# A hybrid decoder layer on one core: SBUF tiles moved by 96 bytes on the left and by 32 bytes on the right

## The chip, the cores and the metric

The kernel runs on one core of a Trainium2 chip. The metric is the device time of one execution, in microseconds. TensorE (PE, with its weight loads shown apart as PEld), VectorE (DVE), ScalarE (ACT) and GpSimd (POOL) compute; SyncE (SP) issues most DMAs.

## The reference

One decoder layer for 1,024 rows of 1,024 numbers in float32:

```
x = x + 0.5 * swiglu(rms_norm(x, g_ffn1), w1_gate, w1_up, w1_down)     # inner width 2816
h = rms_norm(x, g_mix);  proj = h @ w_in                               # one combined projection
y_a = top-k sparse attention: indexer scores, 256 keys of each row, softmax, latent values
y_b = stick-breaking attention (cumulative sums instead of a softmax)
x = x + (sigmoid(g_a) * (y_a @ w_o_a) + sigmoid(g_b) * (y_b @ w_o_b)) @ w_out
x = x + 0.5 * swiglu(rms_norm(x, g_ffn2), w2_gate, w2_up, w2_down)
swiglu(h, g, u, d) = (silu(h @ g) * (h @ u)) @ d
```

## The kernel before, in words

A float32 product is made of three TensorE products: each operand is split into a high part and the rest, and high by high, high by rest and rest by high are added up in PSUM. Most of the work is of one form, a matmul of 128 x 128 numbers that are loaded as weights (the stationary operand, a slice of 512 bytes of each partition) by 512 columns that stream past them (the moving operand, 2,048 bytes of each partition). There are 8,196 of them among the 10,460 matmuls. While one matmul streams, the weights of the next are loaded.

The stages in order are: the first feed-forward block, its entry (`ffn_in`, matmuls at L463 to L465) and its exit (`ffn_out`, L672 to L674); the projections and both attentions, woven together by a planner (L226 to L1950; transposes and products of many shapes); the output projections; and the second feed-forward block by the same two functions. In the feed-forward blocks both products are made by a Strassen scheme on half matrices: `ffn_in` makes seven products of 12 matmuls for each pair of column blocks and each of gate and up, so the loop is seven products of 12 matmuls, over and over, with sums between them on VectorE.

Where a tile lies in SBUF is set by pools. Each partition is filled from both ends: a pool opened with `side="right"` takes its bytes below the last right pool, the others take theirs above the last left one. Pools of small tiles come first on the left (`cst`, `small`), and each small tile takes 32 bytes or a multiple. Nearly all large tiles are of 2,048 or 4,096 bytes, so that all of them on one side begin at one place within every 512 bytes. In the program before, the large tiles of the left begin at place 352 (the first at byte 20,320 = 39 x 512 + 352), those of the right at place 480 (the last at byte 225,248 = 439 x 512 + 480). Both places are 32 bytes past a multiple of 64. Four slots of 4,224 bytes on the right begin at 480, 96, 224 and 352: they hold the weights of the latent queries and keys (`wuqh` at 96, `wqih` at 224).

Which side an operand is on follows from its pool. In `ffn_in` the moving operands (`aB`, `aT`) come from the right pool `t1`. The stationary operands come from `op`, which deals out tiles of two pools in turn, four of the right pool `outer` (`wt`, L256 to L257) and five of the left pool `ring1`, nine in a round:

```
op = in_turn((wt, 4), (lambda name: pool.tile([P, 1024], F32R, tag="r", name=name, bufs=NR), NR))
```

In `ffn_out` both operands (`aA` or `aS`, and `aB` or `aT`) come from `op`. The VectorE's tiles `ay`, `as`, `au` come from left pools, `x` of the first block from the right. In the attention stage, score rows, queries and values lie on both sides. PSUM tiles and DRAM tensors lie elsewhere and are no part of this.

Of the kernel before, what the change touches and what calls it, by code (L numbers as in the profile page):

```python
# [10 lines left out]
F32 = mybir.dt.float32  # L11
# [12 lines left out]
P = 128  # L24
# [220 lines left out]
def trunk(ctx, tc, x, positions, g_ffn1, w1_gate, w1_up, w1_down, g_mix, w_in, g_cq, w_uq_a, w_q_idx,  # L245
          g_q_a, g_k_a, w_uv_a, w_o_a, w_o_b, w_out, g_ffn2, w2_gate, w2_up, w2_down, inv_freq, out):
    nc = tc.nc
    cst = ctx.enter_context(tc.tile_pool(name="cst", bufs=1))
    small = ctx.enter_context(tc.tile_pool(name="small", bufs=4))
    dram = ctx.enter_context(tc.tile_pool(name="dram", bufs=1, space=DRAM))  # L250
    outer = ctx.enter_context(tc.tile_pool(name="outer", bufs=1, side="right"))

    def rawt(name):
# [11 lines left out]
        return small.tile([P, n], dt, name=name, bufs=bufs)  # L265


    ident = cst.tile([P, P], F32, name="ident")
    make_identity(nc, ident)
    mhalf = cst.tile([P, H], F32, name="mhalf")  # L270
# [1836 lines left out]
```

## Time and profile before

| | us |
|---|---|
| median of 3 runs | 2323.19 (2322.38 to 2325.25) |
| the profiled execution | 2324.09 |
| its span, first to last instruction | 2322.3 |
| PE busy in the span | 2211.2 |
| DVE, ACT, POOL busy | 1590.9, 1114.3, 881.6 |

The profiled execution is one run of the program; its span leaves out about 1.8 us around the first and the last instruction. In the rows below a group of instructions stands with its line, engine, operation and tiles (output <- inputs, buffer numbers left out), and then with times. A matmul's own duration contains the time that its last columns take through the array, so a row of matmuls overlaps: its pace is read from the starts, or from how many fill a stretch.

### The profile page before, as it was taken

How to read it: one execution, taken by the hardware profiler on the slowest of the kernel's cores; microseconds unless marked ns; L12 is line 12 of the kernel's file. 1: busy time of each engine (PE TensorE's matmuls, PEld its weight loads, DVE VectorE, ACT ScalarE, POOL GpSimd, SP SyncE). 2: the span in 40 equal slices, each digit the busy share in tenths (PEclk: the TensorE clock that was granted, in tenths of full speed). 3: DMA queues.
4: the chain of work that ended last, by engine and by line, in shares of the span. 5: the costliest groups of instructions: out<-in, count | busy, mean ns of one | idle time of the engine just before them, and what ended most of it. 6: DMA issues, size and time to landing. Idle time of an engine off the chain costs nothing.

```text
span 2322.3 us, 30186 instructions
## 1 busy us (share of the span) xinstructions
PE 2211.2 (95%) x10460; PEld 1811.4 (78%) x10460; DVE 1590.9 (69%) x2512; ACT 1114.3 (48%) x2133; POOL 881.6 (38%) x648
## 2 busy tenths in 40 slices
PE   7999999999999898889999699999999999999999
PEld 6788888878879777667788578877878888888877
DVE  5765656678862897666698877862476565667685
ACT  4323232334452479889988456633342323233443
POOL 3555555432252444211122133146245555542233
PEclk9999999999999999999999799999999999999999
DMA  5232323587664243645454533357313333358755
GB/s 165 75 114 91 114 87 116 159 307 241 168 208 116 81 132 98 163 98 128 109 138 120 172 109 97 128 178 254 118 59 109 96 107 98 105 163 291 234 168 181
DMA packets 252538, 330.64 MB, mean 142 GB/s; under 512 B 20577, under 2 KB 155377, under 8 KB 252385
## 3 DMA queue, kind: packets, MB, share of 16 engines
q1 hardware_dynamic: 235264, 288.83, 41.4%
q0 software_dynamic: 7488, 24.16, 2.7%
q10 hardware_dynamic: 9632, 15.73, 2.0%
q8 instruction: 82, 1.34, 0.2%
q14 instruction: 72, 0.58, 0.1%
HBM read 234.78 MB, written 93.88 MB: 142 GB/s over the span
## 4 chain that ended last, share of the span: by engine, by line
PE 70%; DVE 11%; ACT 9%; DMA 4%; issue 4%; POOL 1%; ACTq 0%; SPq 0%; DVEq 0%; POOLq 0%
PE p L673 5%; PE p L674 5%; PE p L672 5%; ACT junka L1127 4%; PE pc L463 3%; PE pc L465 3%; PE pc L464 3%; PE pd L465 3%; PE pd L463 3%; PE pd L464 3%; PE pa L463 3%; PE pa L465 3%; PE pa L464 3%; PE pb L463 2%; PE pb L465 2%
## 5 line engine op out<-in xcount | busy, mean ns | idle before, releaser
L1127 ACT ACTIVATE junka<-u,cand,sig 128x1024 bf16<-128x1024 f32 (+5 forms) x186 | 182.7, 982 | 22.1 <-DVE cand L1124 10.0
L1563 DVE TENSOR_TENSOR_SCAN left<-left 128x640 f32<-128x640 f32 (+3 forms) x64 | 92.7, 1449 | 3.8 <-ACT left L1555 3.8
L1612 DVE TENSOR_TENSOR pt<-pstT,pt 128x512 fp32r<-128x512 f32 (+1 forms) x96 | 51.3, 551 | 22.0 <-ACT pt L1610 21.4
L1664 PE MATMUL pstT<-ident,sa 128*128 128x128 f32 x288 | 47.4, 279 | 13.7 <-DVE pt L1612 12.0
L1729 DVE CUSTOM_DVE_ANT_0 e<-psL,bias 128x512 f32<-128x512 f32 (+3 forms) x96 | 49.4, 549 | 14.4 <-PE psL L1766 14.4
L1612 DVE TENSOR_TENSOR pt<-pspT,pt 128x512 fp32r<-128x512 f32 x72 | 46.5, 683 | 18.2 <-ACT pt L1610 18.2
L1741 ACT ACTIVATE e<-e,nm 128x256 f32<-128x256 f32 (+7 forms) x64 | 49.4, 774 | 18.5 <-DVE nm L1736 17.3
L1820 PE MATMUL pspT<-ident,e 128*128 128x128 f32 x288 | 42.0, 285 | 16.2 <-DVE ri L1743 9.2
L1566 DVE TENSOR_TENSOR sa<-sa,left 128x639 f32<-128x639 f32 (+3 forms) x64 | 53.1, 829 | 5.0 <-ACT sa L1557 1.8
L1664 PEld LDWEIGHTS pstT<-ident,sa 128*128 128x128 f32 x288 | 35.1, 142 | 26.2 <-DVE pt L1612 17.5
L673 PE MATMUL p<-bT,bS 128*128 128x512 f32 x132 | 51.8, 392 | 2.7 <-DVE bT L374 2.7
L1631 POOL DMA_DIRECT2D ybld<-yl x16 | 8.8, 551 | 118.8 <-DVE yl L1629 66.3
L1610 ACT ACTIVATE pt<-pspT 128x512 fp32r<-128x512 f32 x72 | 39.5, 596 | 29.8 <-PE pspT L1820 29.5
L673 PE MATMUL p<-aT,aS 128*128 128x512 f32 x132 | 51.8, 393 | 1.1 <-DVE aT L374 1.1
L1820 PEld LDWEIGHTS pspT<-ident,e 128*128 128x128 f32 x288 | 35.3, 146 | 22.5 <-DVE e L1744 9.5
L674 PE MATMUL p<-bT,bS 128*128 128x512 f32 x132 | 51.5, 393 | 0.8 <-POOL bS L374 0.8
L1610 ACT ACTIVATE pt<-pstT 128x512 fp32r<-128x512 f32 (+1 forms) x96 | 46.7, 501 | 11.6 <-PE pstT L1664 10.0
L1476 DVE SCALAR_TENSOR_TENSOR u<-relu,WI,u 128x512 f32<-128x512 f32 (+1 forms) x70 | 49.5, 727 | 3.9 <-ACT relu L1469 2.7
L674 PE MATMUL p<-aT,aS 128*128 128x512 f32 x132 | 50.9, 393 | 0.0
L1557 ACT ACTIVATE sa<-psz 128x512 f32<-128x512 f32 (+2 forms) x96 | 47.0, 503 | 5.0 <-ACT evg L1060 2.4
L1555 ACT ACTIVATE left<-psz 128x512 f32<-128x512 f32 (+2 forms) x96 | 45.4, 497 | 8.4 <-PE psz L1590 3.0
L1469 ACT ACTIVATE relu<-psdot 128x512 f32<-128x512 f32 (+1 forms) x80 | 40.0, 521 | 16.5 <-DVE u L1476 10.6
(3061 smaller groups left out, 8315.3 us busy)
## 6 DMA issues: line engine op xcount, KB each, us to landing
aw<-in_w_down_dram SPq DMA_DIRECT2D x33, 512.0 KB, 4.6
bw<-in_w_down_dram SPq DMA_DIRECT2D x33, 512.0 KB, 4.5
a0r<-in_w_gate_dram SPq DMA_DIRECT2D x22, 512.0 KB, 4.2
a1r<-in_w_up_dram SPq DMA_DIRECT2D x22, 512.0 KB, 4.7
b0r<-in_w_gate_dram SPq DMA_DIRECT2D x22, 512.0 KB, 4.1
b1r<-in_w_up_dram SPq DMA_DIRECT2D x22, 512.0 KB, 4.9
x<-in_x_dram SPq DMA_DIRECT2D x16, 512.0 KB, 6.5
gd<-evg ACTq DMA_DIRECT2D x32, 256.0 KB, 2.9
```

What stands on the lines that cost most here:

```text
L463: nc.tensor.matmul(ps, a[:, c], b[k][:, HI], start=start and k == 0, stop=False, skip_group_check=True)
L464: nc.tensor.matmul(ps, a[:, c], b[k][:, LO], start=False, stop=False, skip_group_check=True)
L465: nc.tensor.matmul(ps, a[:, l], b[k][:, HI], start=False, stop=k == 3, skip_group_check=True)
L672: nc.tensor.matmul(ps[q][m], S[:, h], T[:, HI], start=p == 0, stop=False)
L673: nc.tensor.matmul(ps[q][m], S[:, h], T[:, LO], start=False, stop=False)
L674: nc.tensor.matmul(ps[q][m], S[:, l], T[:, HI], start=False, stop=p == last)
L1127: nc.scalar.activation(junks[1][:, 0:(i + 1) * P], score[i], AF.Sign, scale=sig[:, b:b + 1], bias=cand.bitcast(F32)[:, b:b + 1], accum_out ...
L1563: nc.vector.tensor_tensor_scan(back, back, back, 1.0, op0=ALU.mult, op1=ALU.bypass)
L1610: nc.scalar.activation(pt[:, off:512], tp[:, off:512], AF.Copy)
L1612: nc.vector.tensor_sub(pt[:, 512 + off:1024], tp[:, off:512], f32(pt[:, off:512]))
L1664: nc.tensor.transpose(tp[:, q * P:(q + 1) * P], A[n + q][:, j * P:(j + 1) * P], ident)
L1820: nc.tensor.transpose(tp[:, q * P:(q + 1) * P], E[n + q][:, j * P:(j + 1) * P], ident)
```

## The change

Two unused tiles are allocated before all others. On the right one of 8 numbers (32 bytes of each partition) ahead of pool `outer`; on the left one of 24 numbers (96 bytes) as the first of `cst`. Nothing reads or writes them. All left tiles move up by 96 bytes, all right tiles down by 32. The large tiles of both sides then begin at place 448 within 512 (352 + 96, and 480 - 32), a whole multiple of 64. The small left tiles, which follow each other at 32 bytes, move by the same 96; the slots of 4,224 bytes on the right go to 448, 64, 192 and 320. Every engine's instructions, their order and their waits are those of before; their SBUF addresses alone differ.

```
@@ -248,6 +248,8 @@
     cst = ctx.enter_context(tc.tile_pool(name="cst", bufs=1))
     small = ctx.enter_context(tc.tile_pool(name="small", bufs=4))
     dram = ctx.enter_context(tc.tile_pool(name="dram", bufs=1, space=DRAM))
+
+    ctx.enter_context(tc.tile_pool(name="edge", bufs=1, side="right")).tile([P, 8], F32, name="edger")
     outer = ctx.enter_context(tc.tile_pool(name="outer", bufs=1, side="right"))
@@ -265,6 +267,7 @@
         return small.tile([P, n], dt, name=name, bufs=bufs)
 
+    cst.tile([P, 24], F32, name="edgel")
     ident = cst.tile([P, P], F32, name="ident")
     make_identity(nc, ident)
```

## Rows read from the trace of the kernel before

**Rows 1.** The page: span, and busy time of each engine.
```profile
span 2322.3 us, 30186 instructions
PE 2211.2 (95%) x10460; PEld 1811.4 (78%) x10460; DVE 1590.9 (69%) x2512; ACT 1114.3 (48%) x2133; POOL 881.6 (38%) x648
```

**Rows 2.** The page: the chain that ended last, shares by engine.
```profile
PE 70%; DVE 11%; ACT 9%; DMA 4%; issue 4%; POOL 1%; ACTq 0%; SPq 0%; DVEq 0%; POOLq 0%
```

**Rows 3.** Windows by stage: stretch, its length, busy us (and instructions) of engines, DMA.
```profile
0.00:120.00 120.00, 103.25 (x493) 85.14 (x494) 80.39 (x107) 51.06 (x90) 49.33 (x44) 1.00 0.41 122
120.00:462.60 342.60, 342.60 (x1485) 279.16 (x1484) 214.05 (x236) 104.04 (x178) 174.96 (x121) 1.00 0.35 113
462.60:689.10 226.50, 223.20 (x981) 180.92 (x980) 178.39 (x253) 103.66 (x182) 76.19 (x49) 1.00 0.72 226
689.10:1655.00 965.90, 885.06 (x4614) 730.68 (x4613) 677.73 (x1400) 625.98 (x1285) 293.89 (x245) 0.97 0.46 134
1655.00:1715.00 60.00, 60.00 (x312) 50.45 (x311) 36.60 (x50) 24.10 (x44) 18.50 (x14) 1.00 0.16 49
1715.00:2095.60 380.60, 378.03 (x1637) 307.33 (x1636) 245.03 (x267) 114.17 (x196) 198.63 (x137) 1.00 0.36 115
2095.60:2322.30 226.70, 219.03 (x949) 177.71 (x947) 158.69 (x205) 91.23 (x160) 70.12 (x42) 1.00 0.66 219
```

**Rows 4.** Instructions by tile: one product, two rounds; count, ns min/median/max, first and last start.
```profile
L463 PE MATMUL pb<-aT,a04S x4: 392/394/404, 202.2 to 204.3; 128*128 128x512 f32 x4
L464 PE MATMUL pb<-aT,a04S x4: 390/394/404, 202.4 to 204.5; 128*128 128x512 f32 x4
L465 PE MATMUL pb<-aT,a04S x4: 392/394/397, 202.7 to 204.8; 128*128 128x512 f32 x4
...
L463 PE MATMUL pb<-aT,a14S x4: 389/389/389, 221.6 to 223.6; 128*128 128x512 f32 x4
L464 PE MATMUL pb<-aT,a14S x4: 389/389/389, 221.8 to 223.9; 128*128 128x512 f32 x4
L465 PE MATMUL pb<-aT,a14S x4: 389/389/396, 222.0 to 224.1; 128*128 128x512 f32 x4
```

**Rows 5.** Windows of unbroken rows of matmuls: length, PE busy (matmuls), clock, DMA.
```profile
2276.48:2287.42 10.95, 10.95 (x49) 1.00 0.47 146
2287.42:2298.62 11.19, 11.19 (x49) 1.00 0.99 351
...
324.10:332.23 8.13, 8.13 (x36) 1.00 0.60 177
1840.62:1848.75 8.13, 8.13 (x36) 1.00 0.61 179
1538.42:1559.97 21.55, 21.55 (x96) 1.00 0.43 135
507.99:513.58 5.59, 5.59 (x25) 1.00 1.02 389
513.58:521.82 8.24, 8.24 (x37) 1.00 0.95 318
```

**Rows 6.** Windows of two rows of matmuls with 256 columns.
```profile
689.28:700.68 11.39, 11.39 (x97) 1.00 0.79 271
759.13:762.72 3.59, 3.59 (x32) 1.00 0.11 24
```

**Rows 7.** Instructions by tile: matmuls of the latent queries, both operands on the right.
```profile
L306 PE MATMUL psq<-wuqh,cql x16: 388/392/404, 800.8 to 928.4; 128*128 128x512 f32 x16
...
L306 PE MATMUL psq<-wqih,cql x12: 387/389/395, 763.2 to 852.0; 128*128 128x512 f32 x12
```

**Rows 8.** Instructions by line: sums on DVE, tiles on either side.
```profile
L431 DVE TENSOR_TENSOR ay<-x,ay x8: 679/682/684, 39.5 to 55.9; 128x512 f32<-128x512 f32 x8
...
L431 DVE TENSOR_TENSOR ay<-ay,ay x4: 678/682/682, 61.4 to 63.2; 128x512 f32<-128x512 f32 x4
L431 DVE TENSOR_TENSOR ay<-x x4: 678/679/679, 63.8 to 65.6; 128x512 f32<-128x512 f32 x4
```

**Rows 9.** Instructions by tile: splits on ACT and POOL, tiles on either side.
```profile
L373 ACT ACTIVATE a02A<-a0r x3: 615/632/634, 101.0 to 110.9; 128x512 fp32r<-128x512 f32 x3
L374 POOL TENSOR_TENSOR a02A<-a0r,a02A x3: 1291/1304/1307, 102.5 to 111.6; 128x512 fp32r<-128x512 f32 x3
```

**Rows 10.** The page, DMA issues: weights of the two blocks, us to landing.
```profile
a0r<-in_w_gate_dram SPq DMA_DIRECT2D x22, 512.0 KB, 4.2
...
b0r<-in_w_gate_dram SPq DMA_DIRECT2D x22, 512.0 KB, 4.1
```

**Rows 11.** Timeline of PE: every third matmul of the key projection; start, us.
```profile
728.80 0.28 PE L304 MATMUL pska<-wka0h,mhi 128*128 128x264 f32 x1
...
729.17 0.28 PE L304 MATMUL pska<-wka0h,mhi 128*128 128x264 f32 x1
...
729.53 0.28 PE L304 MATMUL pska<-wka0h,mhi 128*128 128x264 f32 x1
...
729.89 0.28 PE L304 MATMUL pska<-wka1h,mhi 128*128 128x264 f32 x1
```

More of the change, by code (lines that the diff above doesn't have):

```diff
@@ L250, in trunk @@
     dram = ctx.enter_context(tc.tile_pool(name="dram", bufs=1, space=DRAM))
+    ctx.enter_context(tc.tile_pool(name="edge", bufs=1, side="right")).tile([P, 8], F32, name="edger")
     outer = ctx.enter_context(tc.tile_pool(name="outer", bufs=1, side="right"))
@@ L265, in sm @@
         return small.tile([P, n], dt, name=name, bufs=bufs)
+    cst.tile([P, 24], F32, name="edgel")
     ident = cst.tile([P, P], F32, name="ident")
```

## The prediction

> **What bounds the kernel now.** I read the busy times first: PE is busy 95% of the span, the next engine 69% [rows 1]. Then the chain of waits that ended last: 70% of it is PE, 4% DMA [rows 2]. Then the same by stage [rows 3]. The reader is to see that PE has no gap at all in the entry of the first feed-forward block after its opening (342.60 of 342.60 us), next to none in that of the second (60.00 of 60.00, 378.03 of 380.60), and few in the exits (223.20 of 226.50, 219.03 of 226.70). Only in the attention stage does it stand still for long (80.8 of 965.9 us). So in 1,236 of 2,322 us the time is the number of matmuls by the pace at which they follow each other, and whatever changes that pace changes the time. The granted clock is at its upper level (1.00) in all of these stages, so the pace isn't the clock's.
>
> The pace isn't constant. One product of `ffn_in`, with the same moving tiles, lasts 389 ns a matmul in one round and 392 to 394 in another [rows 4]. The sole difference is the tile of the stationary operand: in the built program `a14S` of this product starts at byte 208,864 (place 480 within 512, as the moving tiles), `a04S` at 32,608 (place 352). Longer rows say it with starts. In the exit of the second block, 48 matmuls with both operands at one place fill 10.95 us, 228.1 ns each; the next 48, with operands 128 apart, 11.19 us, 233.1 ns (a window counts one matmul more, whose end reaches into it) [rows 5]. The other windows there are pairs against the DMAs: 35 matmuls 128 apart take 232.3 ns at a DMA share of 0.60 or 0.61, 36 at one place 228.9 ns at 0.95, 24 apart 232.9 ns at 1.02, 95 at one place 226.8 ns at 0.43. So it's the place and not the traffic.
>
> Is it the side or the place? The two latent-query products answer: all their operands are on the right. `wuqh` is at 96 and `cql` at 480, 384 apart, and the median matmul takes 392 ns; `wqih` is at 224, 256 apart, 389 ns [rows 7]. So 0 and 256 apart are the fast distances, 128 and 384 the slow ones, on either side. I laid the trace's matmuls beside the built program's addresses, in order: over all rows without a gap, 226 or 227 ns is the commonest interval at 0 or 256 (mean 228.4 ns of some 4,500), and hardly ever occurs at 128 or 384 (mean 232.5 of 3,355). An interval is also slow when only the next matmul's weights, loaded while this one streams, are apart.
>
> **The change part by part.** Instructions, order and waits stay, so nothing is added on any queue and no wait is new. All that can change is how long an instruction or transfer takes at its new address.
>
> 1. Matmuls of 512 columns. After the change both sides are at place 448, so every pair of large tiles is 0 apart. Intervals that are slow now, counted in program order by the places of the two operands and of the next weights: 1,111 in the first entry, 347 in the first exit, 518 between the blocks, 1,123 and 352 in the second entry and exit, 3,451 of 8,195. Each loses what divides the two means of its stage: 4.3 ns in the entries, 4.3 in the exits (232.6 less 228.3), sizes that lie between those of [rows 4] and [rows 5], and 2.6 between. That is 4.8, 1.5, 1.3, 4.8 and 1.5 us, 13.9 us of PE time. A few pairs of `psq` stay 128 apart (both on the right, moved alike); they aren't worth a term.
>
> How much of it reaches the end: in the first entry all but the opening's share (225 slow intervals before 120 us, 1.0 us, half of which I leave to the waits there), 4.3; in the second 4.6 of 4.8; in the exits 1.3 each, as PE stands still for 3.3 and 7.7 us there and a wait for a load eats what comes before it; between the blocks 0.5 of 1.3, since there ACT and DVE hold much of the chain. Sum 12.0 us. What is late next in the entries? Nothing near: DVE is busy 214 of 342.6 us there, POOL 175, DMA 0.35 [rows 3], and 3.4 us less changes that by 1%.
>
> 2. Matmuls of 256 columns and transposes: nothing. 96 matmuls with operands 384 apart fill 11.39 us (118.7 ns), 30 at one place 3.59 us (119.6) [rows 6]; at 256 columns distance costs nothing.
>
> 3. DVE, ACT and POOL: nothing. Sums whose inputs lie on two sides take 682 ns at the median, on the left alone 682, on the right alone 679 [rows 8]; the splits, written to either side, spread by 19 and 16 ns [rows 9]. The small tiles swap places (those at 32 past a 64 go to whole 64 and the others the reverse), half of them in each class as now.
>
> 4. DMAs: no large transfer of before starts at whole 64, so this has no row. DMA holds 4% of the chain, 93 us [rows 2]. Two equal sets of loads land in 4.2 and 4.1 us [rows 10]; that much (2.4%) of 93 us is 2.2 us either way. I take 0, as most of it is hidden, and keep both ends.
>
> 5. Place 448 itself. Two operands at one place give the same pace at 352 as at 480, but both are 32 past a 64. Bounds: the best product runs at 226.8 ns throughout [rows 5], so if all went so, another 1.6 ns x 8,195 x 0.87 (the share that reaches the end in 1) = 11.4 us would go; if all went at the slow pace, 4.1 ns x 4,744 x 0.87 = 16.9 us would come on top of now. I take the present mean: the key projection steps its moving operand through places 0, 32 and 64 past, every second at whole 64, and three matmuls take 0.37, 0.36 and 0.36 us [rows 11].
>
> The profiled execution took 2324.09 us, 0.90 above the median. 2324.09 - 12.0 = 2312.1; for the median 2323.19 - 12.0 = 2311.2 us.
>
> A rule speaks against all this. The Trainium skill, "SBUF — State Buffer", section "Who interferes with whom", gives PE two read ports, one for the moving operand and one for the weights, independent of each other, and says that PE never waits on anyone; by it the place of the two can't matter and the sum is 0, 2323.2 us. The trace disagrees for 512 columns (228.1 and 233.1 ns) and agrees for 256 (118.7 and 119.6); the measurement decides.
>
> **The rivals.**
>
> A. The pace doesn't depend on the place but on something that goes with it, say the distance of the bytes or the pool, and stays: 2323 us, within 2. For it: nearly all slow pairs are left with right. Against it: the pairs on the right alone, 384 and 256 apart, and fast pairs that lie 100 KB from each other (`aT` at 90,080 to 200,672 with `a14S` at 208,864 [rows 4]). The rule of the Trainium skill above would give this time as well.
>
> B. Slower: whole 64 is a bad place for PE to read two streams from. It decides in the feed-forward blocks: if matmuls at one place ran above 230.2 ns, the mean of now over both kinds (4,744 x 228.4 + 3,451 x 232.5, over 8,195), all would be lost; at 232.5 the time is 2323.2 + 16.9 = 2340 us. For it: no row has both 512-column operands there. Against it: rows 11, and the equal pace at 352 and 480.
>
> C. PE gains, and waits take more of it: staged loads and PSUM readers in the exits and the attention come when they come, the exits and everything between give nothing, and of the entries two thirds: 6 us, 2317 us. For it: the idle time of the exits [rows 3]. Against it: the first entry's 342.60 of 342.60.
>
> D. More: the slow intervals left at one place (231 to 236 ns) go as well, 2311.2 - 11.4 = 2300 us. Nothing speaks for it but that 64 is a rounder place.
>
> **How the numbers follow.** Forecast 0.75 (2307 to 2315: 16.1 us off, which is 13.9 with the DMA's 2.2, to 8, two thirds of 12.0), A 0.10, B 0.05, C 0.07, D 0.03. A measurement of this kernel tells 0.2% from no change, 4.6 us. Faster by more: the forecast, C and D, 0.85; within 0.2%: A, 0.10; slower: B, 0.05. The range takes the forecast and C and some way to the others: 2304 to 2319.
>
> **What would show it.** In the profile after, `pb<-aT,a04S` at a median of 389 like `a14S`, and the window of the 48 matmuls that took 11.19 us at 10.95; PE busy lower by some 12 us at the same count; the first entry's 342.6 us shorter by 3.4 or more; 256-column rows, DVE, ACT and POOL groups as now. The forecast is wrong if the 392 to 394 stay (A), if rows that stood at 389 rise (B), or if PE's busy time falls and the span doesn't (C).

## The result, and the profile after

The changed kernel takes 2302.22 us (median of 4 runs, 2298.46 to 2305.05); the kernel before, run beside it, took 2323.34 us (2322.38 to 2325.25). The ratio is 0.9907 (95% interval 0.9890 to 0.9924): 21 us faster, where the forecast was 12 us and its range ended at 2304.

The page of the changed kernel, span, busy times and the chain's shares, against [rows 1, 2]:

```profile
span 2298.7 us, 30186 instructions
PE 2188.0 (95%) x10460; PEld 1808.7 (79%) x10460; DVE 1590.1 (69%) x2512; ACT 1111.9 (48%) x2133; POOL 883.6 (38%) x648
...
PE 67%; DVE 12%; ACT 10%; DMA 5%; issue 5%; POOL 1%; ACTq 1%; SPq 0%; DVEq 0%; POOLq 0%
```

The counts are the same, PE's busy time fell by 23.2 us and the span by 23.6. No other engine's busy time moved by more than 2.4 us. So the gain is PE's own, and in these two executions all of it reached the end.

The windows by stage, cut at the starts of the same matmuls that begin the stages of [rows 3]:

```profile
0.00:119.06 119.06, 101.83 (x494) 85.00 (x495) 79.56 (x106) 50.94 (x90) 49.44 (x44) 1.00 0.41 123
119.06:455.20 336.14, 336.14 (x1484) 278.60 (x1483) 216.86 (x236) 103.09 (x178) 176.07 (x121) 1.00 0.37 115
455.20:678.08 222.88, 220.23 (x981) 181.03 (x980) 179.47 (x253) 103.58 (x182) 77.16 (x49) 1.00 0.73 230
678.08:1639.61 961.53, 881.79 (x4614) 728.25 (x4613) 677.50 (x1400) 625.32 (x1285) 293.72 (x244) 0.97 0.47 135
1639.61:1698.79 59.18, 59.18 (x311) 50.41 (x310) 36.53 (x50) 23.97 (x44) 18.37 (x14) 1.00 0.16 50
1698.79:2072.91 374.12, 371.20 (x1637) 306.85 (x1636) 242.28 (x267) 114.31 (x197) 199.25 (x137) 1.00 0.37 117
2072.91:2298.70 225.79, 217.66 (x948) 178.53 (x946) 157.85 (x205) 90.69 (x160) 69.60 (x42) 0.99 0.67 220
```

Cut at those same matmuls in the trace of before, the stages are 1.2, 6.2, 3.8, 4.3, 0.8, 6.6 and 0.7 us shorter (some cuts lie up to 0.3 us from the round times of [rows 3]). The two entries with their openings give 14.8 us. The second exit gives 0.7 only: its matmuls are faster as well, but PE now stands still for 8.1 us there, and did for 7.7. The waits of PE in that exit, after (engine, line, what it waited for: us in total, times, longest), are 4.1 us; they were 3.5 before:

```profile
PE p L676 <- DVE bT L377: 2.9, 2, 2.6
PE p L677 <- POOL bS L377: 1.0, 1, 1.0
PE p L676 <- DVE bB L377: 0.2, 1, 0.2
```

The product of [rows 4], by tile (count, ns at the least, median and most, first and last start):

```profile
L466 PE MATMUL pb<-aT,a04S x4: 390/390/390, 199.5 to 201.6; 128*128 128x512 f32 x4
L467 PE MATMUL pb<-aT,a04S x4: 389/389/390, 199.7 to 201.8; 128*128 128x512 f32 x4
L468 PE MATMUL pb<-aT,a04S x4: 389/390/390, 200.0 to 202.0; 128*128 128x512 f32 x4
L466 PE MATMUL pb<-aT,a14S x4: 389/390/390, 218.6 to 220.6; 128*128 128x512 f32 x4
```

`a04S`, 392 to 394 ns before, is where `a14S` was all along. More is told by the unbroken rows of [rows 5], the same matmuls after, and below them the two rows of 256 columns [rows 6]:

```profile
2253.67:2264.55 10.88, 10.88 (x50) 1.00 0.49 148
2264.55:2275.43 10.88, 10.88 (x50) 1.00 0.97 343
319.20:327.13 7.93, 7.93 (x36) 1.00 0.64 188
1822.44:1830.37 7.93, 7.93 (x36) 1.00 0.63 188
1521.85:1543.39 21.54, 21.54 (x97) 1.00 0.40 135
499.51:504.95 5.44, 5.44 (x25) 1.00 1.03 399
504.95:513.12 8.17, 8.17 (x38) 1.00 0.84 281
...
678.08:689.59 11.51, 11.51 (x97) 1.00 0.79 268
747.33:750.92 3.59, 3.59 (x32) 1.00 0.21 30
```

The 48 matmuls with operands 128 apart, 11.19 us before, take 10.88; but so do the 48 whose own two operands were at one place before and that took 10.95. By the built program's addresses these 48 weren't all at 480: they went in turns of twelve between 480 and 352, and at each of the three turns the next weights were 128 apart from the moving operand. The rows of 35 go from 8.13 to 7.93, the 36 at one place from 8.24 to 8.17. Only the 95 that stood at 480 from end to end of an unbroken row take what they took: 21.55 and 21.54. Every row now runs at 226.6 to 226.9 ns a matmul, at DMA shares from 0.40 to 1.03. The 96 matmuls of 256 columns rose a little, from 11.39 to 11.51 us.

The mean interval from start to start, over all gap-free rows of 512 columns, worked out from the starts of both traces:

```
                                     before   after
feed-forward, operands apart (2,908)  232.7   226.8
feed-forward, at one place   (2,637)  228.4   226.8
between the blocks, apart             231.6   228.9
between the blocks, at one place      229.1   228.9
```

The latent queries of [rows 7] are a control inside the layer: both operands are on the right and moved alike, so one product stays 128 apart modulo 256 and the other at 0. After the change they take 393 and 390 ns at the median, and the 42 intervals of the first kind have 231.8 ns:

```profile
L309 PE MATMUL psq<-wuqh,cql x16: 389/393/405, 789.0 to 917.1; 128*128 128x512 f32 x16
L309 PE MATMUL psq<-wqih,cql x12: 389/390/627, 751.4 to 840.5; 128*128 128x512 f32 x12
```

### The profile page after: what moved, and what is told of

Its sections match the earlier page's. It is cut to its first block, busy times and chain, and to the rows that moved or that the text cites. A ratio compares the mean times of both kernels' runs of the same rounds, so it can differ in the third digit from the quotient of the medians.

```text
span 2298.7 us, 30186 instructions
## 1 busy us (share of the span) xinstructions
PE 2188.0 (95%) x10460; PEld 1808.7 (79%) x10460; DVE 1590.1 (69%) x2512; ACT 1111.9 (48%) x2133; POOL 883.6 (38%) x648
## 4 chain that ended last, share of the span: by engine, by line
PE 67%; DVE 12%; ACT 10%; DMA 5%; issue 5%; POOL 1%; ACTq 1%; SPq 0%; DVEq 0%; POOLq 0%
PE p L676 5%; PE p L677 5%; PE p L675 4%; ACT junka L1130 4%; PE pc L466 3%; PE pc L467 3%; PE pc L468 3%; PE pd L468 3%; PE pd L466 3%; PE pd L467 3%; PE pa L468 3%; PE pa L466 3%; PE pa L467 3%; PE pb L468 2%; PE pb L467 2%
## 5 line engine op out<-in xcount | busy, mean ns | idle before, releaser
L1744 ACT ACTIVATE e<-e,nm 128x256 f32<-128x256 f32 (+7 forms) x64 | 49.4, 774 | 18.5 <-DVE nm L1739 17.3
```

## The experiments

The diffs are against the changed kernel; "L" and "R" are the places within 512 of the large tiles on the left and the right. In the change both are 448, before L was 352 and R 480. A distance is the stationary operand's place less the moving operand's. The first four ran beside a kernel before of 2319.89 us.

**One place that isn't a whole 64.** L and R at 480.

```
-    ctx.enter_context(tc.tile_pool(name="edge", bufs=1, side="right")).tile([P, 8], F32, name="edger")
...
-    cst.tile([P, 24], F32, name="edgel")
+    cst.tile([P, 32], F32, name="edgel")
```

> Left tiles up by 128 bytes, right tiles unmoved: both sides at place 480, one place but 32 past a whole 64. Theory (distance and whole 64 each count): slow intervals of 512-column matmuls fall from 232.5 to 228.4 ns, those at one place stay at 228.4 with their tail of 231 to 236; 2311 us. Rival 1 (the distance is all): every interval at 226.8 as after the change; 2302 us. Rival 2 (whole 64 is all, the distance nothing): as before, 2323 us.

Measured: 2302.8 us, ratio 0.9919 (0.9903 to 0.9935). The windows of the two rows of 48:

```profile
2256.33:2267.21 10.88, 10.88 (x49) 1.00 0.46 148
2267.21:2278.09 10.88, 10.88 (x49) 1.00 1.00 353
```

Both stand at 10.88 us, as at place 448. I had expected 2311 us; rival 1 held. Whole 64 bytes give nothing, equal places give everything. The fast pace of 226.8 ns is therefore not a property of place 448, and what slowed the row that took 10.95 us before was neither of its two places.

**The right edge alone.** L 352, R 448.

```
-    cst.tile([P, 24], F32, name="edgel")
```

> Only the right edge of 32 bytes: right tiles at 448 (whole 64), left at 352, 96 apart. Theory: pairs on the right alone go from 228.4 to 226.8 ns (some 3,000 of 8,195 matmuls, 4 to 5 us), pairs of both sides stay at 232 to 233; 2318 to 2320 us. Rival 1 (distance is all): pairs of both sides stay slow, those of one side unchanged; 2323 us. Rival 2 (whole 64 of the moving operand is all): all of the entries' matmuls, whose moving tiles are on the right, at 226.8; 2308 us.

Measured: 2324.89 us (10 runs), ratio 1.002 (1.0007 to 1.0033). Matmuls apart follow each other at 233.4 ns, those at one place at 229.5 (right) and 229.7 (left). The product of [rows 4] by tile:

```profile
L465 PE MATMUL pb<-aT,a04S x4: 394/394/394, 201.7 to 203.8; 128*128 128x512 f32 x4
L466 PE MATMUL pb<-aT,a04S x4: 399/399/399, 201.9 to 204.0; 128*128 128x512 f32 x4
L467 PE MATMUL pb<-aT,a04S x4: 390/392/392, 202.2 to 204.3; 128*128 128x512 f32 x4
```

It's no faster than before, and by its ratio 0.2% slower, as the paces are (233.4 and 229.6 against 232.7 and 228.4). The right side stands at whole 64 here and its matmuls at one place run no better than they did, against what I had expected.

**The left edge alone.** L 448, R 480.

```
-    ctx.enter_context(tc.tile_pool(name="edge", bufs=1, side="right")).tile([P, 8], F32, name="edger")
```

> Only the left edge of 96 bytes: left tiles at 448 (whole 64), right at 480, 32 apart. Theory: pairs on the right alone unchanged at 228.4, pairs on the left alone at 226.8 (some 1,000, 1.5 us), pairs of both sides, 32 apart, not measured so far: slow at 232 gives 2322 us, as at one place gives 2310 us. Rival 1 (distance is all, any distance but 0 and 256 slow): 2323 us. Rival 2 (whole 64 of the stationary operand is all): 2313 us.

Measured: 2320.89 us (10 runs), ratio 0.9997 (0.9987 to 1.0008); apart 233.1 ns, at one place 227.5 (right) and 229.0 (left). Neither half does anything by itself, since neither brings the two sides to one place.

**Whole 64 on both sides, 64 apart.** L 384, R 448.

```
-    cst.tile([P, 24], F32, name="edgel")
+    cst.tile([P, 8], F32, name="edgel")
```

> Left up by 32 bytes, right down by 32: left at 384, right at 448, both whole 64 but 64 apart. Theory: pairs on one side at 226.8, pairs of both sides slow by 4 ns or more; 2317 to 2320 us. Rival 1 (distance is all): pairs of one side unchanged at 228.4, others slow, 2323 us. Rival 2 (whole 64 is all): every interval at 226.8; 2302 us.

Measured: 2312.49 us, ratio 0.9954 (0.9937 to 0.9972), half of the change's gain. The windows of the two rows of 48:

```profile
2265.95:2276.91 10.96, 10.96 (x49) 1.00 0.48 147
2276.91:2287.91 11.00, 11.00 (x49) 1.00 0.99 349
```

None of the three expectations had a half. By the starts, the 2,228 intervals with the moving operand on the right and the stationary one on the left (64 less) have 229.2 ns, the 270 with the sides exchanged (64 more) 233.2. So the distance has a sign, which no row of before could show: 128 less and 128 more are the same within 256.

**PE alone, a map of the distances.** No layer: rows of 36 matmuls of 512 columns between two tiles on one side, the moving operand stepped to the place m and the stationary one to m + d, then shorter rows with a few matmuls aside.

```
+        for m in (0, 32, 352):
+            for d in range(0, 512, 32):
+                block([(m, (m + d) % 512)] * 36)
...
+        for d in (32, 64, 96, 128):
+            block(([(0, d)] + [(0, 0)] * 23) * 6)
+            block(([(0, d)] * 12 + [(0, 0)] * 24) * 4)
...
```

> Not the layer: rows of matmuls on numbers of x, no other engine at work, the output is a copy of x. 36 matmuls of 512 columns for each pair of places of the moving and the stationary operand: moving at 0, 32 or 352 past the tile's start, stationary 0 to 480 further in steps of 32, some smaller distances; then rows of one or twelve matmuls apart and 23 or 24 at one place; then 256 and 384 columns. Theory (the distance of the two operands is all): 226.8 ns at distance 0 and 256, 229 to 234 at others, the same curve for all three places of the moving operand; after a single slow pair the intervals of the next nine at one place are some 228 to 229 as well. Rival 1 (whole 64 counts too): the curve at 32 lies above those at whole 64. Rival 2 (what other engines read or write counts): with PE alone all distances take 226.8 ns.

The windows of single rows: first m 0 with d 0, 32, 128, 192 and 256; then m 32 with d 0; then m 352 with d 0 and 128:

```profile
21.44:29.61 8.17, 8.17 (x37) 1.00 0.00 0
29.61:38.00 8.39, 8.39 (x37) 1.00 0.01 2
54.83:63.20 8.37, 8.37 (x38) 1.00 0.01 2
71.59:79.83 8.24, 8.24 (x38) 1.00 0.00 0
88.22:96.39 8.17, 8.17 (x37) 1.00 0.01 2
155.01:163.20 8.19, 8.19 (x37) 1.00 0.00 0
288.60:296.81 8.21, 8.21 (x37) 1.00 0.00 0
322.03:330.40 8.37, 8.37 (x38) 1.00 0.01 2
```

The mean interval from the 13th matmul of each row on, the same for all three m, and beside it the layer's matmuls of the runs above and of the change:

```
d         0      32     64     96     128    160    192    224    (256 to 480: the same again)
ns        226.7  233.4  233.4  234.1  232.7  233.1  228.7  233.3

kernel                          d, moving right / left    map            layer
before                          128 / 128                 232.7          232.7
right edge alone                160 / 96                  233.1 / 234.1  233.4 (both)
left edge alone                 224 / 32                  233.3 / 233.4  233.1 (both)
64 apart                        192 / 64                  228.7 / 233.4  229.2 / 233.2
the change, 480 for both        0                         226.7          226.8
```

PE alone, with no DMA share to speak of and no other engine at work, reproduces these paces of the layer within 0.7 ns. In such rows only the distance within 256 counts; the place itself doesn't, and a side doesn't either.

The same run shows what happens after the last matmul apart. Windows of a row in which twelve matmuls 128 apart (12 starts) are followed by nine at one place and then fifteen more at one place:

```profile
727.31:730.11 2.80, 2.80 (x14) 1.00 0.00 0
730.11:732.18 2.07, 2.07 (x10) 1.00 0.00 0
732.18:735.59 3.41, 3.41 (x17) 1.00 0.00 0
```

That is 233, 230 and 227 ns a matmul. The nine have nothing wrong in their places, and seven of them are still long: an interval isn't slow for its own distance alone but for those before it too. After a single matmul with its weights 128 aside, though, the tail that I expected didn't come: the one before it takes 232.6 ns, it takes 234.0 itself, and the next is at 226.7 again.

**The change once more, and 384 for both.** These two and the next ran beside a kernel before of 2322.92 us, as did the map. The first is the changed kernel itself, the second:

```
-    ctx.enter_context(tc.tile_pool(name="edge", bufs=1, side="right")).tile([P, 8], F32, name="edger")
+    ctx.enter_context(tc.tile_pool(name="edge", bufs=1, side="right")).tile([P, 24], F32, name="edger")
...
-    cst.tile([P, 24], F32, name="edgel")
+    cst.tile([P, 8], F32, name="edgel")
```

> The change as it is, on the same chip as the next two: both sides at place 448. All theories: 0.991 of before.

> Left up by 32 bytes, right down by 96: both at place 384, whole 64. Theory (distance is all): as the change, 0.991 of before, intervals at 226.8 ns. Rival (the place itself counts beside the distance): differs from the change by over 0.2%.

Measured: 2302.25 us, ratio 0.9908 (0.9893 to 0.9922), and 2302.59 us, ratio 0.9915 (0.9899 to 0.9932); intervals of 226.8 ns in both. 384, 448 and 480 can't be told apart.

**The identity too.** The change, with the identity of the transposes moved from place 224 to 448 by three small tiles that are allocated ahead of it.

```
-    cst.tile([P, 24], F32, name="edgel")
+    gk = cst.tile([P, HD], F32, name="gk")
+    mhalf = cst.tile([P, H], F32, name="mhalf")
+    gcolm = cst.tile([P, ND], F32, name="gcolm")
     ident = cst.tile([P, P], F32, name="ident")
     make_identity(nc, ident)
-    mhalf = cst.tile([P, H], F32, name="mhalf")
+    cst.tile([P, 24], F32, name="edgel")
...
-        t = cst.tile([P, n], F32, name=name)
+        t = gcolm if name == "gcolm" else cst.tile([P, n], F32, name=name)
...
-            gcolm = column(g_mix, ND, "gcolm")
+            column(g_mix, ND, "gcolm")
...
-            gk = cst.tile([P, HD], F32, name="gk")
```

> The change, and the identity of the transposes moved from place 224 to 448 by allocating it behind three other small tiles: now the transposes' operands are at one place too. Theory: the 1,080 transposes of 128 columns keep their 108 to 109 ns, and what follows them in the attention stage (512-column intervals of 229 ns) loses up to 2 ns in some hundreds: 0 to 2 us under the change. Rival: the transposes themselves are slowed by the distance and gain several ns each, 5 us or more under the change.

Measured: 2301.9 us, ratio 0.9907 (0.9892 to 0.9922), the same as the change. The 288 transposes of the scores by line, first of the change, then of this run:

```profile
L1667 PE MATMUL pstT<-ident,sa 128*128 128x128 f32 x288 | 46.7, 276 | 12.1 <-DVE pt L1615 10.3
```

```profile
L1668 PE MATMUL pstT<-ident,sa 128*128 128x128 f32 x288 | 46.6, 276 | 12.3 <-DVE pt L1616 10.5
```

276 ns both times, and PE waits for DVE there; transposes that follow each other without a wait have 109.0 ns from start to start in both runs. This was the one attempt at a better version; it isn't one.

**Which two operands meet.** PE alone again: rows at one place, with every 24th matmul having its moving operand, its weights, or both, aside.

```
+        for d in (32, 64, 96, 128):
+            block(([(d, 0)] + [(0, 0)] * 23) * 6)
+            block(([(0, d)] + [(0, 0)] * 23) * 6)
+            block(([(d, d)] + [(0, 0)] * 23) * 6)
...
```

> Not the layer, as the map before it: rows of matmuls on numbers of x with PE alone, the output is a copy of x. Every 24th of a row of 512-column matmuls has its moving operand 32 to 128 bytes aside, then its stationary one, then both; the other 23 have both at 0. Theory (what counts is the moving operand that streams against the weights that are being loaded for the next): a moving operand aside makes the interval of that matmul long (it streams against weights at 0), weights aside the interval ahead of it, both aside makes the matmul and the one ahead of it long, 232 ns or more. Rival (a matmul's own two operands count): moving or weights aside makes that matmul's own interval long, both aside none. Then 256 columns at all distances: theory and rival: no place of either operand matters, and 113 to 120 ns everywhere, by distance alone.

Windows of 120 matmuls with five of them 128 aside: the moving operand, the weights, both. 120 at 226.7 ns would be 27.20 us:

```profile
323.10:350.33 27.23, 27.23 (x121) 1.00 0.00 0
355.79:383.06 27.27, 27.27 (x121) 1.00 0.00 1
388.56:416.05 27.49, 27.49 (x121) 1.00 0.00 1
```

A matmul whose own two operands agree, but differ from its neighbours', is the dearest at 128: 27.49 - 27.20 = 0.29 us for five, 58 ns each, against 6 ns for the moving operand alone and 14 for the weights alone. At 32, 64 and 96 both aside cost 20 to 32 ns each, worked out in the same way, and are nowhere free. So a matmul's own pair isn't all that decides. By the starts (means of five, ns):

```
128 aside          matmul before   itself   the next ones
moving operand     226.6           234.4    225.6
weights            232.6           234.0    226.8
both               233.0           230.0    235.0  230  234  236
```

At 128, aside weights lengthen the matmul before them, during which they are loaded, and an aside moving operand doesn't: there the moving operand that streams meets the weights that are being loaded for the next matmul, as I expected. The other distances, with the weights alone aside, don't all bear this out:

```
weights aside   matmul before   itself   the next ones
32              235.0           228.0    232    231    227
64              226.0           236.0    228    233    231    226
96              228.2           230.8    236    228.2  232.4  231    226.6
```

At 32 the matmul before is the long one; at 64 it isn't, and the time is lost later. The layer has the same pattern in the feed-forward blocks. Intervals in which only the next weights are apart have 232.3 ns at 128 (before) and 233.9 at 32 (left edge alone), but 227.6 at 64 (64 apart). Those in which only the own weights are apart have 233.1 ns at 128 (before). So it is shown that a matmul's own pair isn't all that counts, and not shown which pairs count at every distance.

## Why the prediction was right in kind and too small

**What bounds it** held: PE's 23.2 us less of busy time became 23.6 us less of span, and what moves the pace of the matmuls moves the time.

**Step 1, which intervals change.** Right: the 3,451 intervals counted as slow are those that fell most, 128 apart to 0 apart is what did it, and neither whole 64 bytes nor the side has a part. The rule that I weighed, from the Trainium skill, "SBUF — State Buffer", section "Who interferes with whom" (two independent read ports, and a PE that waits on no one), fails on this chip at 512 columns by more than the layer's trace could show: PE alone has 226.7 ns at one distance and up to 234.1 at another. What in the chip ties the two operands to each other, no run here shows.

**Step 1, the size.** This is the step that failed: "Each loses what divides the two means of its stage: 4.3 ns". I took the mean of the intervals at one place, 228.4 ns, for the fast pace. It was the pace of fast matmuls mixed among slow ones, still paying for them. Sorted by how many intervals after the last slow one they come, those of the feed-forward blocks before have these means:

```
nth after a slow one   1      2      3      4      5      6      7      8      9      10 and on
ns                     231.8  228.4  228.9  229.2  228.4  229.1  228.5  227.7  227.2  226.7
```

The true fast pace is that of the tenth and later. So a slow interval of these blocks loses 232.7 - 226.8 = 5.9 ns, not 4.3, and the other kind, for which I had taken nothing, loses 228.4 - 226.8 = 1.6. Put into the same sum: 2,933 slow intervals by 5.9 are 17.3 us (I had 12.6), 2,637 others by 1.6 are 4.2 (I had 0), and 518 between the blocks by 2.7 are 1.4 (1.3). That makes 22.9 us, and PE's busy time fell by 23.2.

The clue stood in [rows 5]: the only row with no operands apart in it or just ahead of it, 95 matmuls at place 480, ran at 226.8 ns, and the 48 that I had read as "both operands at one place" ran at 228.1. That reading was too simple. By the starts, the first eight of the 48 follow a row 128 apart and lose 38 ns to it, and each of the three turns between 480 and 352 loses 9 or 10; the others are at 226 and 227. I saw the number 226.8, and used it as a bound for step 5 in place of asking what the two rows differ in.

**Step 1, how much reaches the end.** I let 12.0 of 13.9 us through. The runs have no loss in sum (23.2 of busy time and 23.6 of span), but the stages differ: it is 7.4 us in the first entry with the opening (4.3 forecast), 3.8 in the first exit (1.3), 4.3 between the blocks (0.5), 7.4 in the second entry (4.6) and 0.7 in the second exit (1.3). Only the last did what I feared of a stage with waits. Between the blocks the slow intervals account for 2.5 us and rows of 256 columns for 2.0, both with the waits in them; which waits shrank there I haven't separated.

**Step 2.** Nearly right: the transposes didn't gain, also not with the identity at place 448. 256 columns did not gain where nothing waits: 96 of them went from 118.7 to 119.9 ns, a loss of 0.1 us. PE alone has the same sign there (below), so "distance costs nothing" was not quite so.

**Steps 3 and 4** held: DVE's busy time changed by 0.8 us, ACT's by 2.4, POOL's by 2.0, and the loads of [rows 10] land in 4.3 and 4.1 us.

**Step 5, place 448 itself.** The step took nothing for it, and nothing it was: 384, 448 and 480 give the same time. **Rival D** named nearly the right time, 2300 us, for the wrong reason. It expected the slow intervals left at one place to go because 64 is a rounder place; they went, but because the slow intervals ahead of them had gone, and they go at 480 too. (In the sums, 0.87 of step 1 is 0.86, and the 230.2 ns of rival B is 230.1; neither moves the forecast.) Rivals A, B and C fell: the 392 to 394 are 390, no row of 512 columns rose, and the span fell as much as PE's busy time.

## What to carry to other kernels

Where PE has no gaps, compare the start-to-start pace of the same product in two rounds before looking for waits: a difference of 2% that follows a tile's address is worth 1% of the kernel for two unused tiles. When two kinds of instructions are mixed, the mean of the better kind isn't its pace; take that from a long row in which it stands alone. And weigh a layout by the distance, modulo 256, between the moving operands and the weights: either edge alone, or both at whole 64 but 64 apart, gave nothing or half.

## What the runs showed that I had not expected

- The pace of 512-column matmuls depends on the distance modulo 256 and on its sign: 226.7 ns at 0, 228.7 at 192, 232.7 to 234.1 at the other multiples of 32. Close is no help: 4 bytes apart have 232.3 ns, 16 have 233.3.
- One matmul out of place slows others that aren't: single ones 32, 64 or 96 aside lengthen two to seven after them; at 128 a single moving operand or single weights lengthen none, a single matmul with both aside ten, and a run of twelve with the weights aside seven (236, 224, 231, 236, 228, 232, 231 ns before 226.7 comes back). The trace shows that and not its cause, which stays open.
- At 384 columns the same order holds at smaller size: 173.3 ns at distance 0 and 192, 176.7 at 64. At 256 columns it turns about: 120.0 ns at 0, the slowest, and 117.3 at 96, again with a period of 256. One row breaks the period: in the map, 320 apart, 256 columns took 113.3 ns, the fastest of all, and in the other run of PE alone 117.8, as 64 apart. So at 256 columns the distance alone doesn't fix the pace, and what does stays open. In this kernel that would be worth having only if the 256-column operands could be moved without the others, which wasn't tried.
